# Two encoder layers on one core: the convolution's last step, the gate product and the third union sum written to PSUM, and the first group of seven products in another order

## The chip, the cores and the metric

One core of a Trainium2 chip runs the whole program. The metric is the device time in microseconds of one execution; a profiled execution gives the trace from which the profile is read. Engine names in the profile: PE is TensorE's matmul, PEld its weight load, DVE is VectorE, ACT is ScalarE, POOL is GpSimd, SP is the queue that issues the DMAs.

## What is computed

Two layers over x of shape 512 tokens x 1024 features in float32. Each layer has three attention and pooling branches with an output projection (not touched here) and then a gated MLP:

```
hf = rms_norm(x, ffn_norm_g[l])
u  = depthwise_conv(hf @ ffn_w_up[l], ffn_conv_w[l], ffn_conv_b[l])   # width 3 along the tokens
u_gate, u_val = u[..., :D_FF], u[..., D_FF:]                          # D_FF = 2816
x  = x + (silu(u_gate) * u_val) @ ffn_w_down[l]
```

The convolution is centred: output t is w0*u[t-1] + w1*u[t] + w2*u[t+1] + bias, for each channel by itself.

## The kernel before

**Layout.** Activations lie feature-major: 128 features on the partitions, 512 tokens along the free axis. Every float32 operand of a matmul is split into a high and a low float32r part (hi = rounded copy on ScalarE, lo = value - hi on VectorE or GpSimd), and a product is three matmuls: hi x hi, hi x lo, lo x hi.

**The MLP** has 22 chunks of 128 channels (c), each with a gate part ("g", part 0) and a value part ("v", part 1). They are done in two stages (HALVES: chunks 0 to 9, then 10 to 21), each an up stage followed by a down stage over its chunks. The order in the up stage is written out in UPS; in the first stage it is 0g 0v 1g 1v 2 3g 3v 4 5g 5v 6 7g 7v 8 9g 10g 9v. A "g" or "v" alone is a plain projection of 24 matmuls of 512 columns into one PSUM bank. A number alone (2, 4, 6, 8, 12, 14, ...; the list UP_SEVEN) is an up step in which gate and value of one chunk are made together by a seven-product scheme (in place of eight) on 2 x 2 blocks, `both` (L1940): four pairs of input features, 21 matmuls of 256 columns for each, into four banks, which VectorE then unites into the two results. The down stage uses the same scheme for a pair of output tiles m, m+1 (`products`, L1879; the matmul is L1903; `unite`, L1964).

**What a chunk goes through** (`up_evac`, L1792), in order: a scaling of the bank by the norm's factor (VectorE, PSUM to PSUM; in the first stage only); w1*u + bias to an SBUF tile a (ScalarE); the w0 step and the w2 step. In plain chunks both are VectorE's scalar_tensor_tensor with one input in PSUM and a in SBUF, written to a. In UP_SEVEN chunks the w0 step is a scaled copy cv on ScalarE, and GpSimd adds it to a after the w2 step ("a<-a,cv" in the profile). Then the bank is freed. A gate part ends in Silu on ScalarE. A value part ends in the product of value and gate: in even chunks (`prod`, L1833) from a and the gate, both in SBUF, to a; in odd chunks (`prod`, L1845) to a newly taken PSUM bank, from which sums and differences with the even chunk are made and split for the down stage.

**The union** of a pair of output tiles (`unite`): four banks b0 to b3 hold partial sums. ScalarE copies half of b1 to SBUF (p1), VectorE makes u2 = p1 + other half of b1 and u3 = u2 + b3 in SBUF, adds b0 and b2 to the residual tiles x0 and x1 in SBUF (XM), GpSimd adds p1 and u2 to x0, and VectorE adds u3, broadcast to both halves, to x1 ("XM<-XM,u" in the profile). The last pair of the second layer has a shorter path (`early`).

**Banks.** PSUM has eight banks: a ring of six (tags acc, ST, AV, two each) for all products of the MLP, and mi and S, which hold the sums of four weight blocks that the seven-product scheme needs. Those sums are made anew for each group of 21 matmuls (`w_seven`, L413): ScalarE copies one block, VectorE makes three sums ("ps_mi<-", "ps_S<-"), ScalarE rounds them to the high half ("wh<-ps_mi"), VectorE makes the low half ("wl<-ps_mi"). The other three blocks are split by ScalarE and by VectorE or GpSimd, whichever `pick` (L463) finds free sooner in the plan, with a handicap on VectorE ("wl<-raw,wh").

**What sets the order.** Each engine runs its instructions in program order. That order is made while the program is built, by a simulated clock (class Clock, L157): each chain of steps is an event list, every step is issued when the step before it ends in the plan, and costs are planned per engine and size. In `took` (L178) a GpSimd operation, and a VectorE operation with no operand in PSUM, are planned to lock each other out. The order of TensorE's matmuls does not depend on the plan; where a bank or an operand is late, TensorE waits.

**Order within a group of 21** (`products`). The seven products have numbers n; q is 0 for hi x hi, 1 for hi x lo, 2 for lo x hi (weights first). Products 1, 2, 4 use the plain weight blocks, 3, 5, 6, 7 the summed ones. They go to banks: 2 and 3 to the first, 1 and 6 to the second, 4 and 5 to the third, 7 to the fourth. In the first group of a step, before:

```
2q0 2q1 2q2 1q0 1q1 1q2 3q0 3q1 6q0 6q1 4q0 4q1 4q2 5q0 5q1 7q0 7q1 3q2 6q2 5q2 7q2
```

Of the kernel before, what the change touches and what calls it, by code (L numbers as in the profile page):

```python
# [42 lines left out]
HALVES = ((0, 10), (10, 22))  # L43
BOTH = 2
PLAIN = 2
UPS = {0: "0g 0v 1g 1v 2 3g 3v 4 5g 5v 6 7g 7v 8 9g 10g 9v", 10: "10v 11g 11v 12 13g 13v 14 15g 15v 16 17g 17v 18 19g 19v 20 21g 21v"}

def _ups(c0, c1):
# [264 lines left out]
def trunk(ctx: ExitStack, tc: tile.TileContext, x, w, prm, gb, cst, pad, out):  # L313
# [18 lines left out]
    def slot(name, dt=F32):  # L332
        uid[0] += 1
        t = sp.tile([P, SLOT], dt, tag="s", name=f"{name}_{uid[0]}")
        return t
# [325 lines left out]
    def layer(l, sq, xsrc):  # L661
# [1130 lines left out]
        def up_evac(c, part, acc, tag, scaled):  # L1792
            ci = c + part * FC
            u, a = acc, slot("a")

            def scale():
                V.tensor_tensor(acc, acc, fin["rbc"][:, :T], ALU.mult)

            steps = [
                ([("rbc", G2)], scale),  # L1800
                lambda: A.activation(a[:, :T], u[:, :T], AF.Identity, bias=col(PRM_B + ci),
                                     scale=col(PRM_W1 + ci)),
                lambda: V.scalar_tensor_tensor(a[:, 1:T], u[:, 0:T - 1], col(PRM_W0 + ci), a[:, 1:T],
                                               ALU.mult, ALU.add),
                lambda: V.scalar_tensor_tensor(a[:, 0:T - 1], u[:, 1:T], col(PRM_W2 + ci), a[:, 0:T - 1],
                                               ALU.mult, ALU.add),
                lambda: free(tag)][scaled:]
            if c in UP_SEVEN:
                t = slot("cv")
                steps[-3] = lambda: A.activation(t[:, :T], u[:, :T], AF.Copy, scale=col(PRM_W0 + ci))  # L1810
                steps.append(lambda: G.tensor_tensor(a[:, 1:T], a[:, 1:T], t[:, :T - 1], ALU.add))
            if part == 0:
                def gate():
                    A.activation(a[:, :T], a[:, :T], AF.Silu)
                    gated[c] = a
                    done("gate", l, c)
                chain(*steps, gate)
                return
            p = c // 2
            if c % 2 == 0:  # L1820
                whole[p] = a
                full = l == L - 1 and c >= FC - 2 * PLAIN
                if full:
                    uncut[p] = [place("ah"), place("al")]
                    act[p] = [z[:, :256] for z in uncut[p]]
                else:
                    if p % 2 == 0 or c == HALVES[1][0]:
                        act["half"] = [place("ah"), place("al")]
                    hs_ = slice(256 * (p % 2), 256 * (p % 2) + 256)
                    act[p] = [z[:, hs_] for z in act["half"]]  # L1830
                h, lo_ = [z[:, :T] for z in uncut[p]] if full else act[p]

                def prod():  # L1833
                    V.tensor_tensor(a[:, :T], a[:, :T], gated.pop(c)[:, :T], ALU.mult)
                    done("first", l, p)

                chain(*steps, ([("gate", l, c)], prod), *split(h, lo_, a[:, :T] if full else a[:, :256], eng=G), lambda: done("acth", l, p))
                return
            q = []
            t12, t34 = slot("t12"), slot("t34")  # L1840
            new = [place("ah") for _ in range(6)]
            act[p] += new
            t1, t2, t3, t4 = t12[:, :256], t12[:, 256:T], t34[:, :256], t34[:, 256:T]

            def prod():  # L1845
                q[:] = bank(ring)
                V.tensor_tensor(q[1], a[:, :T], gated.pop(c)[:, :T], ALU.mult)

            def diff(o, h_, y_, op):
                return lambda: V.tensor_tensor(o, q[1][:, 256 * h_:256 * h_ + 256], y_, op)  # L1850

            def end(k):
                return lambda: done("act", l, p, k)

            left2 = [2]

            def qfree():
                left2[0] -= 1
                if not left2[0]:
                    free(q[0])  # L1860

            def turns():
                eng = V if c + 1 == FC else G
                w0 = whole.pop(p)
                chain(diff(t3, 1, w0[:, 256:T], ALU.add), diff(t4, 0, t2, ALU.subtract), qfree,
                      *split(new[4][:, :T], new[5][:, :T], t34[:, :T], eng=eng), end(2), after=0.0)
                chain(*split(new[2][:, :T], new[3][:, :T], t12[:, :T], eng=eng), end(1), after=0.0)
# [11 lines left out]
        def products(right_, banks_, first, late=False):  # L1879
            j = st["use"]  # L1880
            his, los = (lambda z: (z[:2], z[2:]))(wnext())
            (bh, bl), (ah, al), (ch, cl), (dh, dl), kb, ka, kc_, kd = right_
            lo_, hi_ = slice(0, 256), slice(256, T)
            right = {1: (bh, bl), 2: (ah[:, lo_], al[:, lo_]), 3: (ah[:, hi_], al[:, hi_]), 4: (dh[:, hi_], dl[:, hi_]),
                     5: (ch[:, lo_], cl[:, lo_]), 6: (ch[:, hi_], cl[:, hi_]), 7: (dh[:, lo_], dl[:, lo_])}
            bank_ = {2: (0, 0), 3: (0, 1), 1: (1, 0), 6: (1, 1), 4: (2, 0), 5: (2, 1), 7: (3, 0)}
            left_ = {1: (0, 2), 2: (0, 0), 3: (1, 3), 4: (0, 1), 5: (1, 0), 6: (1, 2), 7: (1, 1)}
            from_ = {1: kb, 2: ka, 3: ka, 4: kd, 5: kc_, 6: kc_, 7: kd}
            seen = set()
            work = [(n, q) for n in ((2, 1, 3, 6, 5, 4, 7) if late else (2, 1, 4)) for q in range(3)]  # L1890
            if not late:
                work += [(n, q) for n in (3, 6, 5, 7) for q in range(2)] + [(n, 2) for n in (3, 6, 5, 7)]
            if first and not late:
                work = [(n, q) for n in (2, 1) for q in range(3)] + [(n, q) for n in (3, 6) for q in range(2)]
                work += [(4, q) for q in range(3)] + [(n, q) for n in (5, 7) for q in range(2)] + [(n, 2) for n in (3, 6, 5, 7)]
            for n, q in work:
                b, at_ = bank_[n]
                i, k = left_[n]
                need(from_[n], ("wa", j) if i == 0 else ("wh", j) if q < 2 else ("w", j))
                if b not in banks_:  # L1900
                    banks_[b] = bank(ring)
                ws = slice(k * P, k * P + P)
                PE.matmul(banks_[b][1][:, 256 * at_:256 * at_ + 256], lhsT=(his, his, los)[q][i][:, ws], rhs=right[n][q == 1],  # L1903
                          start=first and b not in seen, stop=False, skip_group_check=True)
                seen.add(b)
                ck.to(ck.now + 0.12)
# [57 lines left out]
        def unite(m, banks_, then, early=False):  # L1964
            x0, x1 = XM[:, m, :], XM[:, m + 1, :]
            (t0, b0), (t1, b1), (t2, b2), (t3, b3) = (banks_[n] for n in range(4))
            u, v = slot("u2"), slot("u3")
            p1, u2, u3 = u[:, :256], u[:, 256:T], v[:, :256]
            hi_ = slice(256, T)
            def pair(z):  # L1970
                return z.rearrange("p (a b) -> p a b", a=2)
# [4 lines left out]
            chain(lambda: A.activation(p1, b1[:, :256], AF.Copy), after=0.0)  # L1976
            if early:
                chain(add(x0, x0, b0), add(u2, p1, b1[:, hi_]), add(x0[:, hi_], x0[:, hi_], b2[:, hi_]), add(x0, x0, u[:, :T]),
                      add(x1, x1, b2), add(u3, u2, b3[:, :256]),
                      lambda: V.tensor_tensor(pair(x1), pair(x1), u3[:, None, :].to_broadcast([P, 2, 256]), ALU.add), after=0.0)  # L1980
                return
            chain(add(x0, x0, b0), lambda: free(t0), add(u2, p1, b1[:, hi_]), lambda: free(t1),
                  add(x0[:, hi_], x0[:, hi_], b2[:, hi_]), add(x1, x1, b2), lambda: free(t2),
                  add(u3, u2, b3[:, :256]), lambda: free(t3),
                  add(x0, x0, u[:, :T], G), lambda: then and then(m),
                  lambda: V.tensor_tensor(pair(x1), pair(x1), u3[:, None, :].to_broadcast([P, 2, 256]), ALU.add),
                  lambda: then and then(m + 1), after=0.0)

        def plain(m):
# [260 lines left out]
```

## Time and profile before

| what | value |
|---|---|
| median of 3 runs | 1542.81 us |
| lowest and highest of the 3 | 1536.57 and 1543.53 us |
| the profiled execution's own time | 1542.66 us |
| its span, first to last instruction | 1540.9 us |
| mean granted TensorE clock | 0.999 |
| HBM read, written | 159.89 MB, 22.02 MB |

The span is 1.8 us shorter than the profiled execution's own time; that remainder lies around the instructions. Busy times in the profile are sums of an engine's instruction times; the "idle before" of a group is the idle time of its engine just before its instructions, with what ended most of it. In a timeline row the first number is the start from the span's beginning, the second the duration, both in us. The name "out<-in" is a tile and what it was made from, with buffer numbers left out; a chunk's tile and the gate's tile are both called a, so "a<-a,a" is an even chunk's product of value and gate, and "ps_ST<-a,a" an odd chunk's. MLP stages in the trace: layer 0 from about 432 to 775 us, layer 1 from about 1200 us to the end.

### The profile page before, as it was taken

The numbers are of one execution on the slowest core, as the hardware profiler recorded it, in microseconds if no ns is written. First come the engines' busy times: TensorE is split into PE (matmuls) and PEld (weight loads), VectorE is DVE, ScalarE is ACT, GpSimd is POOL, SyncE is SP. The second block draws the span as 40 slices with busy tenths as digits, with TensorE's granted clock in tenths as the row PEclk, the third lists the DMA queues.
The fourth block names the chain that finished last, engine by engine and source line by source line (L and its number), as shares of the span: only waits on it lengthen the run. The fifth ranks groups of instructions, "written<-read, shape, count | busy, mean of one in ns | idle before, by whom it ended". The sixth has DMA issues, their size and how long they took to land.

```text
span 1540.9 us, 25065 instructions
## 1 busy us (share of the span) xinstructions
PE 1520.5 (99%) x8390; PEld 1326.8 (86%) x8390; DVE 1222.1 (79%) x2343; ACT 973.8 (63%) x1961; POOL 1127.6 (73%) x1076
## 2 busy tenths in 40 slices
PE   9999999999999989999999999999999999999999
PEld 8888788788888889999998887887888888989998
DVE  6778889986578896878956788899865788868786
ACT  6557776664566665666645587866635666756763
POOL 4865986854689886766688659869556998967663
PEclk9999999999999999999999999999999999999999
DMA  6432234434344444333434322344253344533342
GB/s 218 118 110 78 76 96 137 127 93 132 114 138 131 143 151 124 98 109 96 143 125 127 117 68 82 99 140 125 77 153 105 128 150 137 191 111 96 96 122 84
DMA packets 91954, 183.56 MB, mean 119 GB/s; under 512 B 21936, under 2 KB 43696, under 8 KB 91824
## 3 DMA queue, kind: packets, MB, share of 16 engines
q1 hardware_dynamic: 91680, 181.94, 38.2%
q8 instruction: 66, 1.08, 0.3%
q14 instruction: 64, 0.52, 0.1%
q10 hardware_dynamic: 144, 0.01, 0.0%
HBM read 159.89 MB, written 22.02 MB: 118 GB/s over the span
## 4 chain that ended last, share of the span: by engine, by line
PE 81%; DVE 7%; POOL 5%; ACT 4%; issue 2%; DMA 1%; SPq 0%; POOLq 0%; DVEq 0%; ACTq 0%
PE ps_acc L490 22%; PE ps_AV L490 16%; PE ps_ST L490 12%; PE ps_acc L1903 10%; PE ps_AV L1903 7%; PE ps_ST L1903 7%; PE ps_S L490 2%; PE ps_mi L490 2%; POOL wl L279 1%; DVE XM L279 1%; DVE nmt L289 1%; POOL qa L279 1%; ACT wh L271 1%; DVE pl L279 1%; POOL oraw L279 1%
## 5 line engine op out<-in xcount | busy, mean ns | idle before, releaser
L279 POOL TENSOR_TENSOR wl<-raw,wh 128x512 fp32r<-128x512 f32 (+3 forms) x486 | 580.6, 1203 | 319.9 <-ACT wh L271 289.7
L271 ACT ACTIVATE wh<-raw 128x512 fp32r<-128x512 f32 (+2 forms) x521 | 291.3, 578 | 19.1 <-PE ps_AV L490 7.4
L490 PE MATMUL ps_acc<-HH,wh 128*128 128x512 f32 x416 | 162.8, 391 | 0.1
L490 PE MATMUL ps_acc<-HL,wh 128*128 128x512 f32 x416 | 162.3, 390 | 0.0
L490 PE MATMUL ps_acc<-HH,wl 128*128 128x512 f32 x416 | 162.1, 390 | 0.0
L490 PE MATMUL ps_AV<-HH,wh 128*128 128x512 f32 x240 | 93.6, 390 | 0.0
L490 PE MATMUL ps_AV<-HL,wh 128*128 128x512 f32 x240 | 93.5, 390 | 0.0
L490 PE MATMUL ps_AV<-HH,wl 128*128 128x512 f32 x240 | 93.4, 389 | 0.0
L490 PEld LDWEIGHTS ps_acc<-HH,wl 128*128 128x128 f32 x416 | 78.1, 188 | 16.6
L490 PEld LDWEIGHTS ps_acc<-HH,wh 128*128 128x128 f32 x416 | 78.2, 188 | 16.4 <-DVE gt L279 0.6
L490 PEld LDWEIGHTS ps_acc<-HL,wh 128*128 128x128 f32 x416 | 78.1, 188 | 15.4
L271 ACT ACTIVATE wh<-ps_mi 128x512 fp32r<-128x512 f32 x79 | 46.9, 594 | 39.9 <-DVE ps_mi L279 36.1
L490 PE MATMUL ps_ST<-HH,wh 128*128 128x512 f32 x184 | 71.7, 390 | 0.0
L490 PE MATMUL ps_ST<-HL,wh 128*128 128x512 f32 x184 | 71.7, 390 | 0.0
L490 PE MATMUL ps_ST<-HH,wl 128*128 128x512 f32 x184 | 71.6, 389 | 0.0
L271 ACT ACTIVATE wh<-ps_S 128x512 fp32r<-128x512 f32 x79 | 47.0, 595 | 35.9 <-DVE ps_S L279 27.5
L279 DVE TENSOR_TENSOR wl<-ps_S,wh 128x512 fp32r<-128x512 f32 x79 | 54.1, 685 | 12.1 <-ACT wh L271 10.7
L279 DVE TENSOR_TENSOR wl<-ps_mi,wh 128x512 fp32r<-128x512 f32 x79 | 54.1, 684 | 11.6 <-ACT wh L271 10.3
L271 ACT ACTIVATE gt<-gt 128x512 f32<-128x512 f32 x48 | 30.1, 628 | 42.3 <-DVE gt L279 39.9
L1903 PE MATMUL ps_AV<-ah,wh 128*128 128x256 f32 x282 | 56.9, 283 | 0.0
L1903 PE MATMUL ps_acc<-ah,wh 128*128 128x256 f32 x274 | 54.4, 284 | 2.1 <-ACT wh L271 2.1
L289 DVE TENSOR_REDUCE nm<-ps_S 128x1 f32<-128x512 f32 x64 | 43.6, 682 | 15.2 <-PE ps_S L490 14.7
(552 smaller groups left out, 5326.0 us busy)
## 6 DMA issues: line engine op xcount, KB each, us to landing
raw<-w SPq DMA_DIRECT2D x228, 512.0 KB, 3.6
raw<-w SPq DMA_DIRECT2D x13, 384.0 KB, 3.1
XM<-x SPq DMA_DIRECT2D x16, 256.0 KB, 3.7
back<-hsp SPq DMA_DIRECT2D x16, 256.0 KB, 4.0
back<-tsp SPq DMA_DIRECT2D x16, 256.0 KB, 4.4
dtq<-tr SPq DMA_DIRECT2D x16, 192.0 KB, 1.9
dtk<-tr SPq DMA_DIRECT2D x16, 192.0 KB, 2.0
tf<-dtq SPq DMA_DIRECT2D x48, 64.0 KB, 2.4
```

What stands on the lines that cost most here:

```text
L271: return self.eng.activation(out, in_, func, **k)
L279: return self.eng.tensor_tensor(out, *a)
L289: return self.eng.tensor_reduce(out, in_, *a, **k)
L490: PE.matmul(o, lhsT=lhsT, rhs=rhs, start=start, stop=stop)
L1903: PE.matmul(banks_[b][1][:, 256 * at_:256 * at_ + 256], lhsT=(his, his, los)[q][i][:, ws], rhs=right[n][q == 1], start=first and b not in ...
```

## The change

Three steps write to PSUM in place of SBUF, and the first group has another order.

- *Value part, last convolution step.* The w2 step writes to the bank itself, shifted by one column (it reads columns 1 to 511 and writes 0 to 510); the last column, which has no right neighbour, is copied from a. In UP_SEVEN chunks GpSimd's sum now comes before the w2 step. The bank isn't freed there any more. Gate parts are as before.
- *Product.* Even chunks: a = bank * gate, and then the bank is freed. Odd chunks: bank = bank * gate in place; no new bank is taken.
- *Union.* u3 is written over b3's half; the slot "u3" goes; b3's bank is freed after the add of x1.
- *First group:* 2, 1, 3, 6, 4, 5, 7, each with q 0, 1, 2.

```diff
-            if c in UP_SEVEN:
+            if c in UP_SEVEN and (VAL or not part):
                 t = slot("cv")
+
+                def later():
+                    G.tensor_tensor(a[:, 1:T], a[:, 1:T], t[:, :T - 1], ALU.add)
+
                 steps[-3] = lambda: A.activation(t[:, :T], u[:, :T], AF.Copy, scale=col(PRM_W0 + ci))
-                steps.append(lambda: G.tensor_tensor(a[:, 1:T], a[:, 1:T], t[:, :T - 1], ALU.add))
+                steps.insert(*((len(steps) - 2, later) if part else (len(steps), later)))
+            if part:
+                steps[-2:] = [lambda: V.scalar_tensor_tensor(u[:, 0:T - 1], u[:, 1:T], col(PRM_W2 + ci), a[:, 0:T - 1], ALU.mult, ALU.add),
+                              lambda: V.tensor_copy(u[:, T - 1:T], a[:, T - 1:T])]
...
                 def prod():
-                    V.tensor_tensor(a[:, :T], a[:, :T], gated.pop(c)[:, :T], ALU.mult)
+                    V.tensor_tensor(a[:, :T], u, gated.pop(c)[:, :T], ALU.mult)
+                    free(tag)
...
             def prod():
-                q[:] = bank(ring)
-                V.tensor_tensor(q[1], a[:, :T], gated.pop(c)[:, :T], ALU.mult)
+                q[:] = tag, u
+                V.tensor_tensor(u, u, gated.pop(c)[:, :T], ALU.mult)
...
             if first and not late:
-                work = [(n, q) for n in (2, 1) for q in range(3)] + [(n, q) for n in (3, 6) for q in range(2)]
-                work += [(4, q) for q in range(3)] + [(n, q) for n in (5, 7) for q in range(2)] + [(n, 2) for n in (3, 6, 5, 7)]
+                work = [(n, q) for n in (2, 1, 3, 6, 4, 5, 7) for q in range(3)]
...
-            u, v = slot("u2"), slot("u3")
-            p1, u2, u3 = u[:, :256], u[:, 256:T], v[:, :256]
+            u = slot("u2")
+            p1, u2 = u[:, :256], u[:, 256:T]
...
-                  add(u3, u2, b3[:, :256]), lambda: free(t3),
+                  add(b3[:, :256], u2, b3[:, :256]),
                   add(x0, x0, u[:, :T], G), lambda: then and then(m),
-                  lambda: V.tensor_tensor(pair(x1), pair(x1), u3[:, None, :].to_broadcast([P, 2, 256]), ALU.add),
+                  lambda: V.tensor_tensor(pair(x1), pair(x1), b3[:, None, :256].to_broadcast([P, 2, 256]), ALU.add), lambda: free(t3),
```

VAL is a constant, True. The `early` path of the union gets the same edit of u3.

More of the change, by code (lines that the diff above doesn't have):

```diff
@@ L45 @@
 PLAIN = 2
+VAL = True
 UPS = {0: "0g 0v 1g 1v 2 3g 3v 4 5g 5v 6 7g 7v 8 9g 10g 9v", 10: "10v 11g 11v 12 13g 13v 14 15g 15v 16 17g 17v 18 19g 19v 20 21g 21v"}
@@ L1978, in unite @@
                 chain(add(x0, x0, b0), add(u2, p1, b1[:, hi_]), add(x0[:, hi_], x0[:, hi_], b2[:, hi_]), add(x0, x0, u[:, :T]),
-                      add(x1, x1, b2), add(u3, u2, b3[:, :256]),
-                      lambda: V.tensor_tensor(pair(x1), pair(x1), u3[:, None, :].to_broadcast([P, 2, 256]), ALU.add), after=0.0)
+                      add(x1, x1, b2), add(b3[:, :256], u2, b3[:, :256]),
+                      lambda: V.tensor_tensor(pair(x1), pair(x1), b3[:, None, :256].to_broadcast([P, 2, 256]), ALU.add), after=0.0)
                 return
```

## The prediction, made before the changed kernel was run

> **What bounds the kernel now.** I read the page's busy times first.
>
> ```profile
> span 1540.9 us, 25065 instructions
> ## 1 busy us (share of the span) xinstructions
> PE 1520.5 (99%) x8390; PEld 1326.8 (86%) x8390; DVE 1222.1 (79%) x2343; ACT 973.8 (63%) x1961; POOL 1127.6 (73%) x1076
> ```
>
> TensorE is the bound, and nothing in the diff alters its number of matmuls. So the change can only win back time in which TensorE does not stream, and lose time by making it wait. Busy time overstates streaming, because a matmul's modelled 0.28 us overlaps the next one's, so I counted matmuls instead. The next view gives, for the matmuls of the products' line alone, stretches that run from the first of a stage to the start of what follows; its columns are stretch, length, PE busy (matmuls), weight loads, granted clock, DMA share, GB/s.
>
> ```profile
> 486.00:497.66 11.66, 10.53 (x84) 10.13 (x83) 1.00 0.47 134
> 508.55:520.21 11.66, 10.54 (x84) 10.13 (x83) 1.00 0.46 132
> 536.53:593.16 56.63, 52.50 (x420) 51.74 (x419) 0.97 0.47 149
> 609.51:619.58 10.07, 10.07 (x84) 10.02 (x83) 1.00 0.27 74
> 1254.13:1265.47 11.34, 10.54 (x84) 10.13 (x83) 1.00 0.33 100
> 1276.37:1287.62 11.25, 10.54 (x84) 10.14 (x83) 1.00 0.32 101
> 1303.96:1354.38 50.42, 50.41 (x420) 50.37 (x419) 1.00 0.56 188
> 1475.63:1531.42 55.79, 55.79 (x462) 55.50 (x461) 1.00 0.34 107
> ```
>
> The row at 609.51 is undisturbed: 10.07 / 84 = 0.120 us a matmul. At that pace 420 take 50.35 us and 462 take 55.39. What the others lose: 1.59 and 1.59 (two seven-product up steps of layer 0), 6.28 (layer 0's first down stage; layer 1 does the same 420 with 0.07 lost), 1.27 and 1.18 (the same two up steps in layer 1), 0.40 (the last down stage). Together 12.4 us. That is the most the change can return in these stages: 1542.66 - 12.4 = 1530.3 us.
>
> Then I asked for the cause of each. First layer 0's up step at 486: VectorE's groups in 485 to 490 us (busy, mean ns | idle before, releaser).
>
> ```profile
> L279 DVE TENSOR_TENSOR a<-a,a 128x512 f32<-128x512 f32 x1 | 2.9, 2882 | 0.6 <-POOL a L279 0.6
> L283 DVE SCALAR_TENSOR_TENSOR a<-ps_ST,prm,a 128x511 f32<-128x511 f32 x1 | 0.8, 750 | 0.0
> L279 DVE TENSOR_TENSOR ps_AV<-ps_AV,rbc 128x512 f32<-128x512 f32 x1 | 0.7, 686 | 0.0
> ```
>
> The gate product, with both inputs in SBUF, took 2.88 us, where a 128x512 step with one input in PSUM takes 0.69. Everything VectorE had queued came 2.2 us later, the sums of the next weights among it, and TensorE waited for their high half (timeline):
>
> ```profile
> 495.27 0.59 ACT L271 ACTIVATE wh<-ps_mi 128x512 fp32r<-128x512 f32 x1
> ...
> 495.92 0.38 PE L1903 MATMUL ps_AV<-HH,wh 128*128 128x256 f32 x1 [1.13 <-ACT wh L271]
> ```
>
> The down stage, same view:
>
> ```profile
> 555.25 5.52 DVE L279 TENSOR_TENSOR XM<-XM,u 128x512 f32<-128x512 f32 x1
> ...
> 559.21 1.02 POOL L279 TENSOR_TENSOR wl<-raw,wh 128x384 fp32r<-128x384 f32 x1
> ...
> 562.54 0.50 PE L1903 MATMUL ps_acc<-ah,wh 128*128 128x256 f32 x2 [2.10 <-ACT wh L271]
> ...
> 566.50 0.68 DVE L279 TENSOR_TENSOR XM<-XM,ps_acc 128x512 f32<-128x512 f32 x1
> ...
> 567.24 0.51 PE L1903 MATMUL ps_acc<-sMQ,wh 128*128 128x256 f32 x2 [1.81 <-DVE XM L279]
> ```
>
> The union's add of the third sum, also two SBUF inputs, began at 555.25 and ended at 560.77, half a microsecond after the GpSimd row shown, the last of a run of them, had ended at 560.23. Two waits of TensorE follow from it: one for weights, and one for a PSUM bank that VectorE's late add of x0 still held. The granted clock of 0.97 in that stage alone says that TensorE also restarted slowly.
>
> How common is it? VectorE's groups in layer 0's FFN:
>
> ```profile
> L279 DVE TENSOR_TENSOR a<-a,a 128x512 f32<-128x512 f32 x11 | 13.1, 1190 | 1.4 <-POOL a L279 1.4
> L279 DVE TENSOR_TENSOR XM<-XM,u 128x512 f32<-128x512 f32 x8 | 13.0, 1629 | 0.1
> ...
> L279 DVE TENSOR_TENSOR wl<-raw,wh 128x512 fp32r<-128x512 f32 x7 | 10.2, 1453 | 5.8 <-ACT wh L271 5.8
> ```
>
> Means of 1.19 and 1.63 us against 0.69 unblocked: exactly the steps that the diff moves to PSUM. The weight splits (last row) read two SBUF tensors as well, and stay.
>
> **The change part by part.**
>
> *Third union sum in PSUM.* No instruction more or less; the SBUF slot goes. The add of x1 reads one SBUF tensor and should cost what 566.50 shows, 0.68. At 555.25 that is 4.8 us less on VectorE, more than either wait that followed. Of the stage's 6.28 us I count 6.0 back. The fourth bank is freed later, after GpSimd's add of x0 and the x1 add. The ring has six banks and one output pair takes four, so the next pair starts on two free ones and on the two freed first; the fourth is wanted one pair, over 12 us, later. Cost nothing; without that cover it would be the two adds, about 2 us a pair.
>
> *Gate product.* Eleven a layer read the value from PSUM: 0.69 each. In odd chunks the product used to take a second bank; now the convolution's bank stays, so none more is held. In even chunks the bank is held until the product. At the next seven-product step that bank, the last value chunk's bank and four for the step make six: just enough, with no spare.
>
> *Last convolution step to PSUM.* Same operation, 0.75. For the nine seven-product value chunks a layer it moves behind GpSimd's sum. That sum started late before too, and the product waited for it (0.6 us in the row above), so the wait is not new, but 0.75 us that VectorE did before now comes after. Queued behind that wait on VectorE are the next scaling and the weight sums, for which ScalarE's high halves and TensorE wait.
>
> *One-column copy,* 22 a layer. No row shows it; the nearest are a four-column sum and a one-column memset:
>
> ```profile
> L279 DVE TENSOR_TENSOR vm<-ps_acc,vm 128x4 f32<-128x4 f32 x16 | 1.7, 150 | 0.0
> ```
>
> ```profile
> L309 DVE MEMSET warm<- 128x1 f32 x1 | 0.1, 59 | 0.0
> ```
>
> I take 0.10 us, between 0.06 and 0.15; 44 of them are 2.6 to 6.6 us of VectorE, far less than the blocked time removed.
>
> Put together for layer 0's steps at 486 and 508: after GpSimd's sum came 2.88 us, now 0.75 + 0.10 + 0.69 = 1.54. Saved 1.34 each, 2.7 for both, of 3.18 lost. Layer 1:
>
> ```profile
> 1255.05 1.22 DVE L279 TENSOR_TENSOR a<-a,a 128x512 f32<-128x512 f32 x1 [0.18 <-POOL a L279]
> ...
> 1260.15 1.34 DVE L279 TENSOR_TENSOR ps_ST<-a,a 128x512 f32<-128x512 f32 x1
> ```
>
> Here the even product becomes 1.54 for 1.22, a loss of 0.32, and the odd one 0.69 for 1.34, a gain of 0.65: net 0.33 a step, 0.7 for both. About 0.9 us a step of stall stays there.
>
> *Order of the first group.* The third bank is asked for at the thirteenth matmul instead of the eleventh, 0.24 us later. But the low half of the summed weights is asked for at the ninth instead of the eighteenth, 1.08 us earlier. The tightest place that I found is the first seven-product step of each layer:
>
> ```profile
> 443.91 0.67 DVE L279 TENSOR_TENSOR wl<-ps_S,wh 128x512 fp32r<-128x512 f32 x1
> ```
>
> ```profile
> 443.93 0.28 PE L1903 MATMUL ps_acc<-HH,wh 128*128 128x256 f32 x1
> ```
>
> The ninth starts at 443.93 + 0.96 = 444.89, the low half is done at 444.58: 0.31 us to spare. Cost nothing; where that cover is gone, each microsecond of lateness is one of TensorE, at two places.
>
> Sum: 6.0 + 2.7 + 0.7 = 9.4 us; for the last stage's 0.40 I count nothing. 1542.66 - 9.4 = 1533.3, rounded to **1533**. The profiled execution is 0.15 us below the median of the runs shown, so the same sum holds for both.
>
> **The rivals.**
>
> *The stalls stay, for another reason (1539).* VectorE still splits weights with two SBUF inputs at about 1.45 us. The planner gives it a split when it looks free, and it looks freer now. If four of those land in the four up steps that lose time now, they cost 4 x 1.45 = 5.8, and of the 9.4 only 3.6 remain: 1542.66 - 3.6 = 1539. For: the splits are there. Against: at 609.51 none of them cost anything.
>
> A rule weighs on the same side. The Trainium skill, page "SBUF — State Buffer", section "Who interferes with whom", says that a VectorE instruction with two SBUF inputs contends with a GpSimd one that reads SBUF, and that the later one waits until the first has finished. By it the add at 555.25 waits for one GpSimd operation, about 1 us, and ends near 557; the down stage's loss would then have another cause and stay, and the time would be 1542.66 - 3.4 = 1539.3. The trace disagrees: the add outlasted several GpSimd operations in a row. I follow the trace.
>
> *VectorE waits longer for GpSimd (1552, slower).* The place is the value chunks' last step behind GpSimd's sum; the price is TensorE's wait for the weight sums queued behind it. The seven-product up steps of the second stages have a margin that this shows:
>
> ```profile
> 636.46 0.60 ACT L271 ACTIVATE wh<-ps_mi 128x512 fp32r<-128x512 f32 x1
> ```
>
> ```profile
> 639.12 0.28 PE L1903 MATMUL ps_AV<-HH,wh 128*128 128x256 f32 x1
> ```
>
> Ready at 637.06, used at 639.12: 2.06 us. The step and its copy, moved behind the sum, take 0.85 of it. If the sum also comes 2.2 us later than now, each of these ten steps loses 0.85 + 2.2 - 2.06 = 1.0; the four that wait already lose 2.2 less what they gained, 2 x 0.86 in layer 0 and 2 x 1.87 in layer 1. That is 15.4 us lost against the union's 6.0: 1542.66 + 9.4 = 1552. It decides from a sum about 1.5 us later, where loss and gain are even. Against: the sum's inputs are ready sooner, and GpSimd is itself blocked less.
>
> *The edit does nothing (1542).* If operands in PSUM meet the same blocking, the durations stay. Against: no scaling with one PSUM input stands out from 0.69.
>
> **How the numbers follow.** Forecast 0.55 (1530 to 1536), stalls stay 0.25 (1535 to 1541), slower 0.13 (1545 to 1558), nothing 0.07 (1541 to 1544). A measurement here tells apart about 0.5%, 7.7 us, so "faster" begins below 1535.1: nearly all of the forecast's chance and little of the second, 0.53. Within: 0.34. Slower: 0.13. The range 1529.5 to 1543 holds the first two cases and most of the last.
>
> **What would show it.** In the profile after: the x1 adds at 0.68 to 0.70 with the third sum's PSUM tile as input; gate products at 0.69; the stage of 420 matmuls in layer 0 near 50.5 us; the two up steps of layer 0 below 10.5 and those of layer 1 near 11; granted clock 1.00 in all of them. Wrong if a wait of VectorE for GpSimd's sum grows past 1 us, if a seven-product step waits for a bank, or if the first group waits for a low half.

## The result and the profile after

Median after 1537.91 us (21 runs, 1537.02 to 1539.42), median before on the same chip 1541.78 us (21 runs, 1536.57 to 1544.29). The ratio is 0.9981, 95% interval 0.9973 to 0.9989: by the medians 3.9 us gained where 8.8 were forecast (1541.78 - 1533.0), by the ratio, which is not the quotient of the medians, about 2.9. A second set of 12 runs of the same changed kernel on another chip has its median at 1538.63, where 29 runs of before have theirs at 1536.97: ratio 0.9992 (0.9977 to 1.0007).

Before's own times on the first chip form two groups: 6 of 21 at or below 1538.06, 15 at or above 1541.2, nothing between. On the three chips of the experiments the lower group is the larger one: 55 of before's 93 runs lie at or below 1538.1, 5 between the groups, and the medians are 1536.97 to 1537.41. After has one group 2.4 us wide on the first chip and 3.5 on the other. The profiled execution on which the prediction was built, 1542.66 us, belongs to the upper group.

The profiled execution after took 1538.08 us, 4.58 less than that of before. The page's busy times of after:

```profile
span 1536.3 us, 25158 instructions
## 1 busy us (share of the span) xinstructions
PE 1519.1 (99%) x8390; PEld 1325.6 (86%) x8390; DVE 1206.2 (79%) x2386; ACT 974.5 (63%) x1961; POOL 1120.1 (73%) x1077
```

TensorE is the bound as before, so the stages of the products' line say where time went. After, in the order up step, up step, first down stage, last down stage of layer 0, and the same four of layer 1 (columns: stretch, length, PE busy, weight loads, granted clock, DMA share, GB/s):

```profile
485.75:495.82 10.07, 10.07 (x84) 10.02 (x83) 1.00 0.47 158
506.73:516.80 10.07, 10.07 (x84) 10.02 (x83) 1.00 0.47 157
533.15:585.50 52.35, 50.90 (x420) 50.44 (x419) 1.00 0.49 162
706.75:768.85 62.10, 61.30 (x504) 60.63 (x503) 1.00 0.38 121
1248.12:1258.19 10.07, 10.07 (x84) 10.02 (x83) 1.00 0.40 116
1269.10:1279.36 10.26, 10.26 (x84) 10.08 (x83) 1.00 0.36 113
1295.73:1348.05 52.32, 50.89 (x420) 50.43 (x419) 1.00 0.56 183
1469.30:1526.84 57.54, 56.45 (x462) 55.63 (x461) 1.00 0.35 111
```

One stage of before was not shown yet, layer 0's last down stage:

```profile
714.41:774.88 60.47, 60.47 (x504) 60.42 (x503) 1.00 0.40 128
```

Against 10.07, 50.35, 60.42 and 55.39 undisturbed, after loses 0, 0, 2.0, 1.7, 0, 0.2, 2.0 and 2.15: 8.0 us, where before lost 12.4. The 4.4 between them is nearly all of the 4.58. Three of the eight stages are worse than before: layer 1's first down stage (2.0 for 0.07) and both last down stages (1.7 for 0.05, 2.15 for 0.40).

VectorE's groups in layer 0's FFN, after (busy, mean ns | idle before, releaser):

```profile
L280 DVE TENSOR_TENSOR wl<-raw,wh 128x384 fp32r<-128x384 f32 x6 | 9.3, 1546 | 0.6 <-ACT wh L272 0.6
...
L284 DVE SCALAR_TENSOR_TENSOR ps_acc<-ps_acc,prm,a 128x511 f32<-128x511 f32 x10 | 7.5, 749 | 0.7 <-POOL a L280 0.6
...
L280 DVE TENSOR_TENSOR XM<-XM,ps_acc 128x512 f32<-128x512 f32 x9 | 6.1, 680 | 0.1
...
L280 DVE TENSOR_TENSOR a<-ps_AV,a 128x512 f32<-128x512 f32 x4 | 2.8, 688 | 0.1
```

Adds and products are at 0.68 and 0.69 us and the last convolution step at 0.75. What stands out now is the first row: weight splits, two SBUF inputs, 1.55 us for 384 columns. One of the six is this one, in the timeline of the first down stage after:

```profile
556.08 1.01 POOL L280 TENSOR_TENSOR wl<-raw,wh 128x384 fp32r<-128x384 f32 x1
556.09 3.93 DVE L280 TENSOR_TENSOR wl<-raw,wh 128x384 fp32r<-128x384 f32 x1
...
557.05 2.55 POOL L280 TENSOR_TENSOR tf<-back,tf 128x512 fp32r<-128x512 f32 x2
...
560.47 0.68 DVE L280 TENSOR_TENSOR XM<-XM,ps_AV 128x512 f32<-128x512 f32 x1
...
561.20 0.51 PE L1911 MATMUL ps_AV<-sMQ,wh 128*128 128x256 f32 x2 [1.26 <-DVE XM L280]
...
562.37 0.50 PE L1911 MATMUL ps_AV<-sMQ,wh 128*128 128x256 f32 x2 [0.20 <-DVE u L280]
```

The split begins a hundredth after GpSimd's and ends at 560.02, after three GpSimd operations (the last ends at 559.60). The x0 add, unblocked itself, comes after it, its bank is free at 561.15, and TensorE waits for that bank. Layer 1 repeats it: a split of 3.92 at 1318.66, waits of 1.23 and 0.20. In before the same two splits took this:

```profile
564.66 1.40 DVE L279 TENSOR_TENSOR wl<-raw,wh 128x384 fp32r<-128x384 f32 x1
```

```profile
1327.64 0.90 DVE L279 TENSOR_TENSOR wl<-raw,wh 128x384 fp32r<-128x384 f32 x1
```

The last down stage of layer 0, after, is another matter:

```profile
715.99 0.69 DVE L280 TENSOR_TENSOR ah<-t,ah 128x512 fp32r<-128x512 f32 x1
716.59 0.68 DVE L280 TENSOR_TENSOR ah<-ps_acc,ah 128x512 fp32r<-128x512 f32 x1
717.19 0.68 DVE L280 TENSOR_TENSOR ah<-t,ah 128x512 fp32r<-128x512 f32 x1
...
720.44 0.50 PE L1911 MATMUL ps_ST<-ah,wh 128*128 128x256 f32 x2 [0.22 <-ACT wh L272]
...
721.16 0.39 PE L1911 MATMUL ps_ST<-ah,wl 128*128 128x256 f32 x1 [0.22 <-DVE wl L280]
...
724.79 0.39 PE L1911 MATMUL ps_ST<-sMQ,wh 128*128 128x256 f32 x1 [0.37 <-DVE XM L280]
```

Three low halves that the last chunk's product makes stand in one row on VectorE, ahead of weight sums; TensorE then waits for a high half, a low half and a bank. Before had them apart, with other work between:

```profile
719.67 0.69 DVE L279 TENSOR_TENSOR ah<-t,ah 128x512 fp32r<-128x512 f32 x1 [0.17 <-ACT ah L271]
...
720.61 0.68 DVE L279 TENSOR_TENSOR ah<-ps_ST,ah 128x512 fp32r<-128x512 f32 x1
...
722.14 0.73 DVE L279 TENSOR_TENSOR ah<-t,ah 128x512 fp32r<-128x512 f32 x1
```

### The profile page after: what moved, and what is told of

Read it like the earlier page. It is cut to its first block, busy times and chain, and to the rows that moved or that the text cites. A ratio compares the mean times of both kernels' runs of the same rounds, so it can differ in the third digit from the quotient of the medians.

```text
span 1536.3 us, 25158 instructions
## 1 busy us (share of the span) xinstructions
PE 1519.1 (99%) x8390; PEld 1325.6 (86%) x8390; DVE 1206.2 (79%) x2386; ACT 974.5 (63%) x1961; POOL 1120.1 (73%) x1077
## 4 chain that ended last, share of the span: by engine, by line
PE 75%; DVE 12%; ACT 6%; POOL 3%; issue 3%; DMA 1%; SPq 0%; ACTq 0%; DVEq 0%; POOLq 0%
PE ps_acc L491 24%; PE ps_AV L491 16%; PE ps_ST L1911 8%; PE ps_ST L491 8%; PE ps_acc L1911 7%; PE ps_AV L1911 6%; PE ps_S L491 2%; PE ps_mi L491 2%; ACT wh L272 2%; DVE nmt L290 1%; DVE wl L280 1%; DVE vt L284 1%; DVE XM L280 1%; DVE pl L280 1%; POOL qa L280 1%
## 5 line engine op out<-in xcount | busy, mean ns | idle before, releaser
L491 PE MATMUL ps_acc<-HH,wh 128*128 128x512 f32 x504 | 196.9, 391 | 0.1
L491 PE MATMUL ps_acc<-HL,wh 128*128 128x512 f32 x504 | 196.5, 390 | 0.0
L491 PE MATMUL ps_acc<-HH,wl 128*128 128x512 f32 x504 | 196.3, 389 | 0.0
L491 PEld LDWEIGHTS ps_acc<-HH,wl 128*128 128x128 f32 x504 | 94.6, 188 | 19.9
L491 PEld LDWEIGHTS ps_acc<-HH,wh 128*128 128x128 f32 x504 | 94.7, 188 | 19.7 <-DVE gt L280 0.6
L491 PEld LDWEIGHTS ps_acc<-HL,wh 128*128 128x128 f32 x504 | 94.7, 188 | 18.9
L280 POOL TENSOR_TENSOR a<-a,cv 128x511 f32<-128x511 f32 x36 | 46.8, 1314 | 21.9 <-DVE a L284 21.9
L1911 PE MATMUL ps_ST<-ah,wh 128*128 128x256 f32 x294 | 55.5, 284 | 0.3 <-ACT wh L272 0.2
L272 ACT ACTIVATE ps_ST<-ps_ST 128x512 f32<-128x512 f32 x74 | 42.3, 583 | 20.1 <-PE ps_ST L491 12.4
L491 PEld LDWEIGHTS ps_AV<-HH,wl 128*128 128x128 f32 x248 | 46.6, 188 | 9.8
```

The source lines that it names most:

```text
L272: return self.eng.activation(out, in_, func, **k)
L280: return self.eng.tensor_tensor(out, *a)
L491: PE.matmul(o, lhsT=lhsT, rhs=rhs, start=start, stop=stop)
```

## The experiments

The theory after the result: the blocking of two-input SBUF steps has passed from the x1 add to the next such step on VectorE, the weight split. Rivals: the bank waits come from the changed order of the first group, or from the bank that is held longer. All times are medians of 12 runs unless said; each ratio is to before on the same chip. e1 to e4 ran on one chip, e5 to e7 on a second, e9, e10 and e12 on a third, so medians from different lists are from different chips.

### The change in three parts

e1: before with the union's part alone (the hunk of `unite`). e2: before with the value part alone (the hunks of `up_evac`). e3: before with this line alone:

```diff
-                work = [(n, q) for n in (2, 1) for q in range(3)] + [(n, q) for n in (3, 6) for q in range(2)]
-                work += [(4, q) for q in range(3)] + [(n, q) for n in (5, 7) for q in range(2)] + [(n, 2) for n in (3, 6, 5, 7)]
+                work = [(n, q) for n in (2, 1, 3, 6, 4, 5, 7) for q in range(3)]
```

> The kernel before with the union's edit alone (third sum written over the fourth bank, no slot u3). Theory: the add of x1 takes 0.68 us instead of 5.52 in layer 0's first down stage, so the 6.28 us lost there go, unless the next VectorE instruction with two SBUF inputs (the weight split that stood at 564.66) meets the same run of GpSimd work; then about 2 us of waiting stay in the stage. The four up steps keep their 1.2 to 1.6 us each. Time 1535.5 to 1538. Rival, that VectorE's planned order sets the waits and not the blocking: the stage keeps 4 us or more, and the time stays within 1 us of the kernel before (1541.8).

Measured: 1541.7 us, ratio 1.0015 (0.9997 to 1.0032), where 1535.5 to 1538 was expected. The x1 adds fell to 0.68. Timeline and stages of the two first down stages:

```profile
559.85 3.38 DVE L279 TENSOR_TENSOR wl<-raw,wh 128x384 fp32r<-128x384 f32 x1
```

```profile
536.57:589.07 52.50, 50.90 (x420) 50.44 (x419) 1.00 0.51 162
1299.20:1353.20 54.00, 52.40 (x420) 51.95 (x419) 0.97 0.53 176
```

With the adds out of the way the splits are blocked, in both layers (3.39 at 1322.47 in layer 1). Layer 0 keeps the 2 us of waiting that the expectation allowed for; that layer 1 would now lose 3.6 it had not foreseen. Order and value part are those of before here, so the new order is not needed for these waits. The fourth bank is held longer here too, so that rival stays until e4.

> The kernel before with the value part's edit alone (last convolution step and product in PSUM, one-column copy). Theory: the four up steps (1.59, 1.59, 1.27, 1.18 us lost) lose under 0.3 together, the x1 add in layer 0's first down stage can still be blocked for several us, and the new losses of the last down stages (1.6 us in layer 0, 2.1 in layer 1 after the change) appear here if the plan's new order around chunk 21 makes them: 1541.8 - 5.4 + 3.7 = about 1540. Rival, that those losses come from the new order of the first group: they are absent here, and the time is about 1536.5.

Measured: 1543.87 us, ratio 1.0018 (1.0001 to 1.0034), above the 1540 expected. The profiled execution took 1540.79; in it the four up steps were at 10.07 to 10.09: this part alone removes their stalls. The x1 add at 552.68 took 5.32, and the last down stages lost 2.3 and 2.7: the second new loss comes with the value part. In e1 those stages took 60.61 and 55.94, near before's 60.47 and 55.79.

> The kernel before with the new order of the first group alone. Theory: nothing that was lost depended on it except the wait for the third bank (1.97 us at 567.24, later by 0.24 us of matmuls now), so 1541.5, within 0.5 us of the kernel before. Rival, that the earlier need for low halves makes new waits, or moves the plan: the last down stages lose 1.5 to 2 us more each, and the time is 1544 to 1545.

Measured: 1537.01 us, ratio 0.9994 (0.9974 to 1.0014): the time expected was 1541.5, but before's median on this chip is 1537.27, and within 0.5 us of that it is. The last down stages, 60.47 and 55.43 us, show nothing of the rival. Its profiled execution, 1535.19 us, has before's unions and yet no blocked add:

```profile
553.91 1.09 DVE L279 TENSOR_TENSOR XM<-XM,u 128x512 f32<-128x512 f32 x1
```

The first down stages lost nothing there. So the add that cost 5.5 us in the profile of before need not be blocked, though this program differs from before in TensorE's order; before itself was profiled once. That a blocked add is what parts before's times into two groups is argued from this pair of profiles (5.52 at 1542.66 us, 1.09 at 1535.19), not shown run by run.

### The splits

e4: after, with the plain blocks' splits of the seven-product scheme given to GpSimd always. e7: the same edit in before. e10 repeats e4 beside e9, which is the changed kernel again.

```diff
-            e = pick(W_BIAS)
+            e = G
```

> The changed kernel, with every split of the plain weight blocks of a seven-product group on GpSimd (none on VectorE). Theory: the 3.93 us split at 556.09 and its twin in layer 1 (3.92 us) are what makes TensorE wait 1.41 + 0.36 and 1.39 + 0.36 us for banks; without them both first down stages lose under 0.2 us, the last ones keep their 1.6 and 2.1, and the time is 1537.9 - 3.9 = 1534. Rival, that the banks are late by VectorE's planned order anyway, or that GpSimd is now late with low halves: 1537 or more.

Measured: 1534.22 us (1533.62 to 1535.17), ratio 0.9965 (0.9949 to 0.9981). Stages, in the order first and last down stage of layer 0, then of layer 1:

```profile
532.70:583.09 50.39, 50.39 (x420) 50.34 (x419) 1.00 0.55 178
704.34:767.25 62.91, 61.23 (x504) 60.58 (x503) 1.00 0.38 123
1293.90:1344.29 50.39, 50.39 (x420) 50.34 (x419) 1.00 0.56 188
1465.54:1522.97 57.43, 55.93 (x462) 55.48 (x461) 1.00 0.35 111
```

Both first down stages are clean, with order, banks and unions as in after: the split was the cause of their 4.0 us. Between the medians lie 3.7 (1537.91 - 1534.22, from two chips); the last down stages lose 0.7 more than in after, 2.5 and 2.0.

> The changed kernel again, beside the next two on one chip. Theory: it has one outcome, since its blocked instruction (the split in each first down stage) is blocked in every execution: times within 2.5 us of each other around 1538, while the kernel before spreads over groups some 6 us apart (no x1 add blocked, one, or both). Which of the two is faster by the median then hangs on how many executions of the kernel before fall into the lowest group. Rival, that the chip sets the level: both shift together.

> The kernel of e4_split again, on the chip of the changed kernel's repeat. Theory: faster than that repeat by the two waits of the first down stages, 1.97 + 1.94 = 3.9 us, so near 1534.2. Rival: within 1 us of it.

Measured: e9 1538.63 us, ratio 0.9992 (0.9977 to 1.0007); e10 1535.2 us, ratio 0.9963 (0.9947 to 0.9980). 3.4 us apart again, this time on one chip. The expectation that after's times lie within 2.5 us of each other failed: they run from 1535.77 to 1539.31. e9's profiled execution, at 1539.31, has both blocked splits at their old places (3.94 and 3.90 us) and the same waits of TensorE, 1.27 and 0.20 in layer 0. Yet its first down stage of layer 0 took longer than in after, with a lower granted clock:

```profile
532.88:586.74 53.86, 52.39 (x420) 51.94 (x419) 0.97 0.49 157
```

So these same waits cost 2.0 us in one execution and 3.5 in another.

> The kernel before with every split of a seven-product group's plain blocks on GpSimd, nothing in PSUM. Theory: the products and the x1 adds, two SBUF inputs each, still meet GpSimd's runs: the up steps lose their 1.2 to 1.6 us, and the x1 add is blocked for over 4 us in some executions and not in others: the times spread over two groups some 6 us apart, as those of the kernel before do, near 1536 and 1542. Rival, that the split alone was the fault: narrow times near 1534.

Measured: 1542.55 us, ratio 1.0015 (1.0000 to 1.0031); 3 of the 12 runs lie at 1538.1 to 1538.6 and 9 at 1541.6 or above, a lower group some 2 us above the one expected. The layer 0 products in the steps at 486 and 508 us were still at 2.88 and the x1 add at 566.0 took 3.78. The splits off VectorE gain nothing while other two-input SBUF steps stay on it.

### The order of the first group

e5: after, with the old order of the first group (the diff of e3, reversed).

> The changed kernel with the old order of the first group (value part and union as changed). Theory: the order of the first group only shifts when a late bank is noticed: the blocked split in each first down stage stays (over 3 us) and with the third bank asked for 0.24 us earlier the waits there grow from 1.97 and 1.94 to about 2.2 each; the last down stages keep their 1.6 and 2.1. Time within 1 us of the changed kernel (1538 to 1539). Rival, that the new order itself made the waits of the last down stages: these go and the time falls by 3 us.

Measured: 1542.06 us (1541.34 to 1544.0), ratio 1.0023 (1.0011 to 1.0035): 3.4 to 4.2 us above the two medians of after. My expectation failed. These medians are from different chips, so the 3.4 to 4.2 can hold a difference of chips. Layer 1's first down stage, which with the new order lost 2.0 us at clock 1.00, in e5:

```profile
1323.69 0.39 PE L1912 MATMUL ps_AV<-sMQ,wh 128*128 128x256 f32 x1 [1.48 <-DVE XM L280]
...
1324.86 0.44 PE L1912 MATMUL ps_AV<-sMQ,wh 128*128 128x256 f32 x1 [0.32 <-DVE u L280]
```

```profile
1295.66:1349.85 54.19, 52.39 (x420) 51.94 (x419) 0.97 0.53 175
```

The waits are some 0.25 and 0.1 us longer than after's 1.23 and 0.20, as the later request for the third bank says; the clock is lower, and the stage loses 3.8. But e9 has the new order and the same clock in its layer 0, so the lower clock can't be put down to the order. In layer 0 e5 loses 2.4. In the last down stages 2.4 and 3.8 are lost for after's 1.7 and 2.15 (1.8 and 2.5 in e9). There, too, the bank waits are 0.24 us longer, 0.61 for 0.37 and 0.85 for 0.62, and in layer 1 two waits of 0.2 us for a bank are new. All eight stages together lose 12.4 us in e5, 8.0 in after and 9.8 in e9.

### The last down stage

e6: e4, with two low halves of the last chunk on GpSimd. e12: e4, with the last chunk's convolution and product as in before.

```diff
-                eng = V if c + 1 == FC else G
+                eng = G
```

```diff
-            if part:
+            if part and c + 1 < FC:
...
-                q[:] = tag, u
-                V.tensor_tensor(u, u, gated.pop(c)[:, :T], ALU.mult)
+                q[:] = (tag, u) if c + 1 < FC else bank(ring)
+                V.tensor_tensor(q[1], u if c + 1 < FC else a[:, :T], gated.pop(c)[:, :T], ALU.mult)
```

> The kernel of e4_split, and the low halves of two of the last chunk's sums (chunk 21) made on GpSimd like those of all other chunks. Theory: the waits left in the last down stages (2.4 us in layer 0, 2.0 in layer 1 in e4_split) come from three low halves in a row on VectorE ahead of the weight sums; with two of them on GpSimd, idle for 2 us there, they go: 1534.2 - 4 = about 1530.5. Rival, that the operands of chunk 21 then come too late from GpSimd (1.3 us each instead of 0.68): the waits stay or grow, 1534 to 1536.

Measured: 1537.16 us, ratio 0.9985 (0.9972 to 0.9998). The waits for weight halves went in layer 0 and fell to 0.20 in layer 1, but one longer bank wait in each layer took their place (2.22 in layer 1; layer 0 here):

```profile
724.37 0.39 PE L1911 MATMUL ps_ST<-sMQ,wh 128*128 128x256 f32 x1 [2.38 <-DVE XM L280]
```

Nothing gained; the expectation failed. The stages lose 2.8 and 3.0 us, more than e4's 2.5 and 2.0. In layer 0 the x0 add that frees the bank stood behind a weight's low half on VectorE.

> The kernel of e4_split with chunk 21's value part as in the kernel before (last step to SBUF, bank freed, product into a newly taken bank). Theory: the waits in the last down stages come from where the plan puts chunk 21's three low halves among the weight sums, and that shifted with its product; as before, the stages lose about 0.4 us, and the time is 1534.2 - 3.5 = near 1531. Rival, that these waits come from the rest of the value edit (every value chunk's later finish) or from GpSimd's extra splits: 2 us or more stay there, and the time stays at 1534.

Measured: 1534.23 us (1532.7 to 1534.73), ratio 0.9969 (0.9955 to 0.9984). Its last down stages:

```profile
705.24:766.44 61.20, 61.05 (x504) 60.58 (x503) 1.00 0.39 127
1464.31:1522.54 58.23, 56.85 (x462) 55.74 (x461) 1.00 0.33 109
```

Layer 0 loses 0.8 for e4's 2.5, layer 1 loses 2.8 for 2.0, now mostly as bank waits of 0.62, 0.32 and 0.32 us at the thirteenth matmul of a pair. The time expected was near 1531: the theory, that the last chunk's value part alone makes this loss, holds for most of layer 0's loss and fails for layer 1. What the planner makes of these stages as a whole was not isolated. Of all versions measured, e4 and e12 are the lowest.

### The blocking by itself

e8, e11 and e13 compute nothing of the reference: VectorE adds of 128x512 that start while GpSimd runs, over and over. In e8, GpSimd makes `gate` and then n more operations; VectorE's add waits for `gate` alone. Eight turns of one kind follow eight of the other.

```
for n in (1, 2, 4, 7):
    for kind in ("two", "one"):
        o, y = (two, xc) if kind == "two" else (one, acc)   # acc is in PSUM, the rest in SBUF
        for _ in range(8):
            G.tensor_tensor(gate, xa, last, ALU.add)
            for i in range(n): G.tensor_tensor(run[i]..., xa..., xb..., ALU.subtract)
            V.tensor_tensor(o, y, gate, ALU.add)
```

> Measures the blocking alone; computes nothing of the reference. VectorE adds two 128x512 tensors while GpSimd runs 1, 2, 4 or 7 operations back to back that do not depend on it; the add becomes ready when the run's first operation starts. Eight times each, once with both inputs in SBUF and once with one input in PSUM. Theory from the 5.52, 3.93 and 2.88 us of the traces: with both in SBUF the add can outlast the whole run, so its duration grows with the run's length up to some 8 us at 7; with one in PSUM it stays at 0.69. Rival, the rule that the later instruction waits for the one in progress: about 2 us at most with any run.

Measured groups and, for n = 7, the first two adds in the timeline:

```profile
L342 DVE TENSOR_TENSOR two<-xc,gate 128x512 f32<-128x512 f32 x32 | 66.1, 2065 | 108.5 <-POOL gate L338 108.5
L342 DVE TENSOR_TENSOR one<-ps_acc,gate 128x512 f32<-128x512 f32 x32 | 22.1, 692 | 138.5 <-POOL gate L338 138.5
```

```profile
202.64 8.25 DVE L342 TENSOR_TENSOR two<-xc,gate 128x512 f32<-128x512 f32 x1 [4.88 <-POOL gate L338]
...
212.26 1.73 DVE L342 TENSOR_TENSOR two<-xc,gate 128x512 f32<-128x512 f32 x1 [1.37 <-POOL gate L338]
```

With one input in PSUM, 0.69 every time. With two in SBUF, the first of each eight outlasts the whole run from n = 2 on (2.68 at n = 2, 4.86 at 4, 8.25 at 7), and the other seven take 1.73: they wait for one operation. Both forms of blocking exist; what chooses between them?

> Measures the blocking alone again, with four GpSimd operations after the one that makes VectorE's add ready; computes nothing of the reference. Before that one GpSimd runs 0, 1, 2, 3 or 5 others back to back, and in three more groups of six the add starts 0.13 to 0.6 us later (a short add with one input in PSUM before it). Theory: the add outlasts the whole run (4.9 us) where GpSimd had been running without a pause before it, as in the first add of each group of e8_block, and takes its turn after one operation (1.73) where GpSimd had just waited. Rival, that the start within the running operation decides: the groups with a lag differ from those without, and the number of operations ahead does not matter.

e11 put 0 to 5 GpSimd operations ahead of `gate`, and short PSUM adds ahead of VectorE's. Measured: 1.73 for every number ahead, and 1.60, 1.39 and 1.14 with the PSUM adds, which only means that less of the operation in progress was left. Neither theory nor rival: all took turns.

> Measures the blocking alone a third time; computes nothing of the reference. Four GpSimd operations run after the one that makes VectorE's add of two SBUF tensors ready. Between two such adds stand 0, 1, 2 or 8 adds of VectorE with one input in PSUM, each with its own five GpSimd operations, and in three more groups 5, 10 or 40 more GpSimd operations and no VectorE add; six times each. Theory: an add outlasts the whole run (4.9 us) when VectorE's previous add did not use two SBUF inputs, and takes its turn (1.73) when it did: all groups with ones before are at 4.9, all others at 1.73. Rival: the number of GpSimd operations since VectorE's last two-SBUF add decides: 40 more make it 4.9 too. Second rival: neither; then the first adds of e8_block's groups stay unexplained.

e13 put PSUM adds (each with five GpSimd operations) or plain GpSimd operations between the two-SBUF adds. Measured: with 0 or 1 PSUM adds between, or 5 or 10 more GpSimd operations, 1.73 throughout. With 2 PSUM adds, 4.86 once and 1.73 five times; with 8, 4.86 five times and 10.96 once (five more operations were queued behind that one); with 40 more GpSimd operations, 53.66 and 1.73 in turn:

```profile
751.38 53.66 DVE L342 TENSOR_TENSOR two<-xc,gate 128x512 f32<-128x512 f32 x1 [53.07 <-POOL gate L338]
...
806.41 1.73 DVE L342 TENSOR_TENSOR two<-xc,gate 128x512 f32<-128x512 f32 x1 [1.38 <-POOL gate L338]
```

The kind of VectorE's previous add, my theory, does not decide: with 40 GpSimd operations and no PSUM add the long block came. What fits these three programs is how many operations GpSimd has begun since VectorE's last step with two SBUF inputs. Up to 14 the adds took turns, with one exception at 14 (the 4.86 with 2 PSUM adds); from 18 on (e8's first add with n = 2) they outlasted the run. The 1.73 among the 40s fit too: each starts two GpSimd operations after the long add before it has ended.

In the kernels' traces the count does not decide. After's split at 556.09 had 22 GpSimd operations behind it, e1's at 559.85 had 15, and both were blocked long; before's split at 564.66 came 3.9 us behind the x1 add, itself such a step, and took its turn. But a split of after at 524.32, with 86, took its turn as well: it waited for the GpSimd operation in progress and not for the one that followed at once.

```profile
524.32 1.15 DVE L280 TENSOR_TENSOR wl<-raw,wh 128x384 fp32r<-128x384 f32 x1
```

```profile
523.75 1.30 POOL L280 TENSOR_TENSOR wl<-raw,wh 128x512 fp32r<-128x512 f32 x1 [2.66 <-ACT wh L272]
525.00 1.62 POOL L280 TENSOR_TENSOR a<-a,cv 128x511 f32<-128x511 f32 x1
```

The other way round, the x1 add of e7 at 566.00 was blocked for 3.78 us with 9. With 11 the x1 add went both ways, 5.52 in before's layer 0 and 1.07 in its layer 1, and with 18 in e2, 5.32 and 0.84. What decides in a kernel stays open.

The Trainium skill, page "SBUF — State Buffer", section "Who interferes with whom", says that a VectorE step with two SBUF inputs and a GpSimd step that reads SBUF lock each other out, and the later one waits until the first has finished. The measurements agree for the 1.73 and for the 0.69 with an input in PSUM; they differ at 4.86, 8.25 and 53.66, where the add outlasted the whole run, and there the measurement decides.

## Why the prediction was right or wrong

| part | forecast gain | measured in the two profiles |
|---|---|---|
| layer 0's first down stage | 6.0 | 56.63 - 52.35 = 4.28 |
| layer 0's up steps | 2.7 | 2 x 1.59 = 3.18 |
| layer 1's up steps | 0.7 | (11.34 - 10.07) + (11.25 - 10.26) = 2.26 |
| layer 1's first down stage | 0 | 50.42 - 52.32 = -1.90 |
| last down stages | 0 | (60.47 - 62.10) + (55.79 - 57.54) = -3.38 |
| sum | 9.4 | 4.44 |

- **What held.** TensorE is the bound, and what it loses to waits makes up the terms. The blocked products and x1 adds were the causes of the stalls named: with PSUM operands they are at 0.69 and 0.68, and the up steps at 10.07 (e2 for the products, e1 for the adds).
- **What failed first: "Of the stage's 6.28 us I count 6.0 back".** The row of weight splits was on my list of two-SBUF steps with the remark that they "stay", and I priced one at 1.45 us, as a rival at other places. But before's splits in this stage, 1.40 and 0.90 us, came 3.9 us behind the add, and say nothing of a split that meets GpSimd's run in the add's place. With the adds gone, the split is VectorE's first two-SBUF step in 30 us and is blocked for 3.9 us, in both layers: 1.7 less than forecast in layer 0, 1.9 lost in layer 1. e4 shows it: without these splits on VectorE both stages are clean. It also shows that holding the fourth bank longer cost nothing there, as forecast.
- **What failed second: nothing was counted for the last stages.** The loss there grew by 3.4 us. e2 shows that it comes with the value part, e12 that the last chunk is only part of it. That the three low halves in a row make it is argued from the traces; moving two of them (e6) only put other waits in their place, so how the value part makes this loss stays open.
- **"About 0.9 us a step of stall stays" in layer 1** did not hold, nor did the same step's partial gains in layer 0: 2.0 us more came back than counted (5.44 for 3.4), which hides part of the two misses in the sum. In e2 these steps are clean as well, so it is the value part's doing; which of its steps gave the extra was not isolated.
- **Order of the first group, "cost nothing".** No cost shows. In before it changed nothing (e3), but the changed kernel with the old order is 3.4 to 4.2 us slower by medians from different chips (e5). I weighed the 0.24 us by which the third bank is asked for later at places where banks were not late; here they are, and 0.2 to 0.26 us is added to each wait for a third bank under the old order, 1.4 us over e5's down stages. Nearly the same waits cost 2.4 us in e5's layer 0 and 3.8 in its layer 1, at the lower clock, and that clock can't be put down to the order. The rest was not isolated.
- **One-column copy.** 0.15 us, the upper bound; I took 0.10. The group in layer 0's FFN, after:

```profile
L298 DVE COPY ps_acc<-a 128x1 f32<-128x1 f32 x10 | 1.5, 149 | 0.0
```

- **Rivals.** "The stalls stay" at 1539 came nearest, with the right instruction, but by another route: four splits in up steps at 1.45 each there, two in down stages at 3.9 each here. That the number is near is luck. Its second account, that the down stage's loss has another cause and stays, failed: 4.28 of 6.28 came back. VectorE's longest wait for GpSimd's sum, at 506.56, is 0.59 us, so the slower case did not come up. Of the prediction's signs of being wrong one came: groups of the seven-product scheme wait for banks, in the down stages (1.26 us at 561.20).
- **The base.** I built on one profiled execution and took it for the median. It holds a blocked x1 add and lies in the upper of two groups, to which the 1536.57 among the first three runs was a hint. On the chip where both were run and before's median is 1536.97, the changed kernel can't be told from it.

## What to carry to other kernels

When a lock between two engines is the cause, list all instructions that take it in that stretch and ask which one will be the next to wait: clearing the adds left the split to pay (e1, after), and clearing the split too gave the gain (e4). That an instruction is cheap soon after a blocked one is no evidence that it stays cheap alone. And look at the spread of the times of before: where they form groups, find out to which one the profiled execution belongs before its stalls are counted as gains.

## What the runs showed of the hardware that was not expected

- A VectorE add with two SBUF inputs, started while GpSimd works through a queue, either waits for one operation (1.73 us) or for the whole queue (8.25 us behind 7 operations, 53.66 us behind 44). With one operand in PSUM it took 0.69 us in all 98 adds of e8 and e13.
- In the benchmarks the choice goes with the number of GpSimd operations since VectorE's last such step: one operation up to 14 (with one exception, at 14), the whole queue from 18 on. In the kernels it does not: a step with 86 waited for one operation (1.15 us) and a step with 9 was blocked for 3.78 us. The rule stays open.
- The same step behind the same 11 operations took 5.52 us in before's layer 0 and 1.07 in its layer 1, and 1.09 in e3's layer 0. Whether one and the same program takes either course from one execution to the next was not profiled.
- The same program lost 2.0 us in a stage at granted clock 1.00 and 3.5 at 0.97 in another execution, with waits of TensorE within 0.01 us of each other.
